# Where the low part of a weight chunk starts in its buffer: 128 bytes away, modulo 256, from where the high part starts

## The chip, the cores and the metric

The kernel runs on one core of a Trainium2 chip. The core has a matrix engine (TensorE; in the profile PE for the matmul's stream of columns and PEld for the load of its stationary operand), a vector engine (DVE), a scalar engine (ACT), GpSimd (POOL) and a queue engine that only issues transfers (SP). The metric is the time of one execution on the device, in microseconds; of several executions the median counts.

## The reference

A two-layer model over 512 tokens of width 1024, all in float32. Layer 0 mixes tokens by dilated attention in three groups, layer 1 by an mLSTM; after each comes a SwiGLU feed-forward of inner width 2816. Cut to what matters:

```python
def dilated_attention_mixer(xn, positions, w_in, w_out):
    proj = (xn @ w_in).reshape(B, S, N_GROUPS, 3, ATTN_HEADS, ATTN_HEAD_DIM)   # q, k, v
    ...                                     # rope, windowed softmax per group, groups mixed
    return o.reshape(B, S, ATTN_WIDTH) @ w_out

def mlstm_mixer(xn, w_in, ...):
    proj = xn @ w_in
    ...                                     # conv, gates, chunked recurrence
    return (h * jax.nn.sigmoid(o_pre)) @ w_out

def swiglu(xn, w_in, w_out):
    gu = xn @ w_in
    return (jax.nn.silu(gu[..., :D_FF]) * gu[..., D_FF:]) @ w_out

for i in range(2):
    h = h + (dilated_attention_mixer, mlstm_mixer)[i](rms_norm(h, ...), ...)
    h = h + swiglu(rms_norm(h, ffn_norm[i]), ffn_w_in[i], ffn_w_out[i])
return rms_norm(h, final_norm)
```

Nearly all of the work is the products with the weight matrices.

## The kernel before, in words

**Products in three matmuls.** TensorE takes its operands in a shortened float format (`F32R`). To keep float32 accuracy every operand is split into a high part (a rounded copy, made by ACT) and a low part (the difference, made by DVE), and a product is three matmuls: high by high, high by low, low by high (`SPLITS`, line 47). So each weight chunk of 128 x 1024 numbers has two buffers, tag `whi` for the high part and `wlo` for the low part, three of each in rotation (`W_BUFS`). `split_chunk` (line 227) allocates both and issues the two splitting instructions.

**Where a chunk starts.** The buffers are longer than the chunk by `PAD` = 64 elements (256 bytes per partition), and a chunk starts at an offset in them: `WIDE` = 0, `NARROW` = 16 elements (64 bytes) or `TOKENS` = 48 elements (192 bytes). A buffer is 1088 x 4 = 4352 bytes = 17 x 256 long, so all buffers of a tag start at the same place modulo 256, and the high and the low part of a chunk do too. In the memory plan of the built program that place is 32, and nearly all activation tiles that are streamed start at 32 as well. `WIDE` chunks thus start at 32, `NARROW` ones at 96 and `TOKENS` ones at 224. Every fourth chunk of the attention goes to a spare pair of buffers (`spare`), without padding or offset, whose place in the plan is 96.

**Which products are narrow.** Several large products are done by a seven-product (Strassen-like) scheme on blocks; their operands are half as long, so a matmul has 256 columns and not 512. These are the q and k projections of the attention (`qk_unit`, matmul at line 1055, tiles `a0g1c`, `a1g1u` and so on), the feed-forward's first product in both layers (`products` in `ffn_in`, line 1677, tiles `f0j_c`, `f0j_p`, `f0j_u` in layer 0 and `f1j_*` in layer 1) and its second product in layer 0 (`tile_mm`, line 1993, tile `fo`, weights `f0P`). In all of them the weights are the stationary operand, loaded before each matmul (128 columns of 4 bytes per partition), and the activations are streamed (256 columns of 4 bytes). They use `NARROW`. The mLSTM's v projection (`project_tokens`, line 326, tiles `mv`) streams 256 columns of weights over stationary activations, and uses `TOKENS`. Everything else has 512 columns and uses `WIDE`.

**The order of one triple.** The innermost loop issues, for each k, the matmuls high weights by high activations, high weights by low activations, low weights by high activations. The weights of a matmul are loaded while the matmul ahead of it streams. Beside the first matmul of a triple runs the second load of the high part, beside the second matmul the load of the low part, and beside the third the load of the next high part:

```python
for m in range(2):
    for k in range(4):
        for a, b in SPLITS:       # (0, 0), (0, 1), (1, 0): 0 high, 1 low
            nc.tensor.matmul(acc[name][:, m * HALF:(m + 1) * HALF], whl[a][:, k, m * P:(m + 1) * P],
                             ops[okey][b][:, k], ...)
```

The steps in k and m are multiples of 256 bytes, so modulo 256 each load and each stream starts where its buffer's chunk starts.

**What sets the order.** The program is written out in full: a list of products per stage, with the splits of the chunk that comes two products later issued between them (`AHEAD`). Each engine works its list in order and waits on semaphores. Loads of raw weights are issued by SP and wait for free buffers.

Of the kernel before, what the change touches and what calls it, by code (L numbers as in the profile page):

```python
# [12 lines left out]
F32R = mybir.dt.float32r  # L13
# [4 lines left out]
P = 128  # L18
# [24 lines left out]
           (19, 20, 21))  # L43
LAST_OUTPUTS = {6: 22, 7: 23}
W_BUFS = 3
PAD, WIDE, NARROW, TOKENS = 64, 0, 16, 48
SPLITS = [(0, 0), (0, 1), (1, 0)]


# [27 lines left out]
def tile_hybrid_dilated_attn_mlstm(  # L77
# [5 lines left out]
    x = x[0]  # L83
    out = out[0]

    def pool(stack, name, **kw):
        return stack.enter_context(tc.tile_pool(name=name, bufs=1, **kw))
# [3 lines left out]
    wp = pool(ctx, "w")  # L91
# [116 lines left out]
    spare = []  # L208
    ahead_of_splits = [None]

    def behind_scores():
        return tc.issue_after(ahead_of_splits[0]) if ahead_of_splits[0] is not None else nullcontext()
# [3 lines left out]
    def behind_factors():  # L216
        return tc.issue_after(ahead_of_casts[0]) if ahead_of_casts[0] is not None else nullcontext()
    splits = itertools.count()
# [3 lines left out]
    def run_late(_):  # L222
        while lows:
            with tc.issue_after(last_on(mybir.EngineType.DVE)):
                lows.pop(0)()

    def split_chunk(chunk, at=WIDE):

        raw, n, view, name = chunk
        p, more, bufs = (spare[0], "4", 1) if spare and next(splits) % (W_BUFS + 1) == W_BUFS else (wp, "", W_BUFS)  # L230
        at, pad = (0, 0) if more else (at, PAD)
        hi = p.tile([P, 1024 + pad], F32R, tag="whi" + more, name=name + "_h", bufs=bufs)[:, at:at + 1024]
        lo = p.tile([P, 1024 + pad], F32R, tag="wlo" + more, name=name + "_l", bufs=bufs)[:, at:at + 1024]
        with behind_factors():
            nc.scalar.activation(hi[:, :n], raw[:, :n], AF.Copy)  # L235
        def low():
            nc.vector.tensor_tensor(lo[:, :n], raw[:, :n], hi[:, :n].bitcast(F32), op=ALU.subtract)  # L237
        if late[0]:
            lows.append(low)
        else:  # L240
            with behind_scores():
                low()
        return view(hi), view(lo)

    def split_weights(src, shape, name):
        return split_chunk(load_chunk(src, shape, name))
# [30 lines left out]
    def project(pairs, w2d, c0, nk, evac, name, hook=None, ready=(), amid=False):  # L277

        acc = [acc_tile("%s_%d" % (name, m)) for m in range(2)]
        for ch in range((nk + 3) // 4):  # L280
            n = min(4, nk - 4 * ch)
            whl = ready.pop(0) if ready else split_chunk(weight_chunk(w2d, ch, c0, n, "%s_k%d" % (name, ch)))
            for m in range(2):
                with fenced():
                    multiply(acc[m], whl, pairs, ch, m, nk)
                if 4 * ch + n == nk and hook is None:
                    evac(m, acc[m])
                if amid and (ch, m) == (1, 0):
                    with tc.issue_after(last_on_pe()):
                        run_deferred(lambda t: t <= tick[0] + 1)  # L290
            if 4 * ch + n == nk and hook is not None:
                hook()
                for m in range(2):
                    evac(m, acc[m])
            advance()
# [20 lines left out]
    def project_tokens(pairs, w2d, c0, evac, name, tok=lambda t, tb: t[:, tb * P:(tb + 1) * P]):  # L316

        acc = [acc_tile("%s_%d" % (name, m)) for m in range(2)]
        for ch in range(KC // 4):
            whl = split_chunk(weight_chunk(w2d, ch, c0, 4, "%s_k%d" % (name, ch)), TOKENS)  # L320
            for m in range(2):
                with fenced():
                    for i, k in itertools.product(range(2), range(4)):
                        kk = ch * 4 + k
                        for a, b in SPLITS:
                            nc.tensor.matmul(
                                acc[m][:, i * 256:(i + 1) * 256],
                                tok(pairs[a][kk], 2 * m + i), whl[b][:, k, :],
                                start=(kk == 0 and i == 0 and (a, b) == SPLITS[0]),
                                stop=(kk == KC - 1 and (a, b) == SPLITS[-1]),  # L330
                                skip_group_check=True)
                ends[name] = last_on_pe()
                if ch == KC // 4 - 1:
                    evac(m, acc[m])
            advance()
# [85 lines left out]
    with ExitStack() as actx:  # L421
# [93 lines left out]
            else:  # L515
                nc.scalar.activation(h[k], xps[k], AF.Copy)

        his = [wp.tile([P, 1024 + PAD], F32R, tag="whi", name="first%d_h" % i, bufs=W_BUFS)[:, :1024] for i in range(2)]
        los = [wp.tile([P, 1024 + PAD], F32R, tag="wlo", name="first%d_l" % i, bufs=W_BUFS)[:, :1024] for i in range(2)]
        facc = [ps.tile([P, 512], F32, tag="o", name="a0g0q_%d" % m, bufs=2) for m in range(2)]  # L520

        def v12_parts(pr):
# [953 lines left out]
    def norm(key, k0, name, ssum=None, wait=1):  # L1476
        pair = x_tiles(name)
        add = None
        if ssum is None:
            ssum, add = squares_of(name)  # L1480
        for k in range(KC):
            split_act(pair[0][k], pair[1][k], h[k], col(key, k0 + k))
            if add is not None:
                add(k)
        v = npl.tile([P, TB], F32, tag="rs_v4", name=name + "v", bufs=2)
        box = {}

        def sums():
            sp = ps.tile([P, 512], F32, tag="t", name=name + "ss", bufs=1)
            for tb in range(TB):  # L1490
                nc.tensor.matmul(sp[:, tb:tb + 1], ssum[:, tb * P:(tb + 1) * P], ones[:, 0:1],
                                 start=True, stop=True)
            nc.vector.tensor_copy(v, sp[:, :TB])
            box["finish"]()
        rbc, r, hook = inverse_rms(v, name, box)
        defer(wait, sums)
        return pair, rbc, r, hook
# [253 lines left out]
    def output_products(layer, fp, wo, sums_of_rows):  # L1751
# [7 lines left out]
        narrow = NARROW if sums_of_rows else WIDE  # L1759
# [10 lines left out]
        def subtract(out, x, y):  # L1770
            nc.vector.tensor_tensor(out, x, y, op=ALU.subtract)

        def split_operand(name, u, src):

            i = UNITS * (PARTS.index(name) % 3) + u
            nm = "f%d%s_%d" % (layer, name, u)
            if i < 2 * len(PRODUCTS):
                t = fp.tile([P, 2, 2, HALF], F32R, tag="op%d" % i, name=nm)
                hi, lo = t[:, 0], t[:, 1]
            else:  # L1780
                hi, lo = [fp.tile([P, 2, HALF], F32R, tag="gu0", name=nm, bufs=3) for _ in range(2)]
            nc.scalar.activation(hi, src, AF.Copy)
            subtract(lo, src, hi.bitcast(F32))
            ops[name, u] = [[t[:, k] for k in range(2)] for t in (hi, lo)]
# [18 lines left out]
        def prepare_first_sum(u, own, nm):  # L1803

            view = lambda t: t.rearrange("p (k n) -> p k n", k=2)
            hi = wp.tile([P, 1024 + PAD], F32R, tag="whi", name=nm + "_h", bufs=W_BUFS)[:, narrow:narrow + 1024]
            lo = wp.tile([P, 1024 + PAD], F32R, tag="wlo", name=nm + "_l", bufs=W_BUFS)[:, narrow:narrow + 1024]
            for t, ks in first_sums[u]:
                nc.scalar.activation(view(hi)[:, ks], t, AF.Copy)
                subtract(view(lo)[:, ks], t, view(hi)[:, ks].bitcast(F32))  # L1810
            whl["P5", u] = view(hi), view(lo)
            for t, ks in first_sums[u]:
                subtract(view(own)[:, ks], t, view(own)[:, ks])
            split_operand("P5", u, sums[u])

        def prepare_product(name, u):
# [22 lines left out]
            if sums_of_rows and name == "P5":  # L1839
                prepare_first_sum(u, t, nm)  # L1840
                return
# [98 lines left out]
        first, second = (0, 1) if sums_of_rows else (1, 0)  # L1940
# [6 lines left out]
        for e in order:  # L1947
            name, i = e.split("_")
# [29 lines left out]
    pair, rbc, _, hook = norm("ffn", 0, "n1", ssum)  # L1978
# [62 lines left out]
    with ExitStack() as mctx:  # L2041
# [142 lines left out]
        i = 0  # L2184
# [165 lines left out]
    pair, rbc, _, hook = norm("ffn", KC, "n3", ssum)  # L2350
# [224 lines left out]
```

## Time and profile before

| | |
|---|---|
| time, median of 3 runs (lowest to highest) | 1358.64 us (1357.73 to 1359.58) |
| the profiled execution: its own time | 1359.36 us |
| its span, first to last instruction | 1357.6 us |
| TensorE clock granted, mean | 0.998 |
| matmuls recorded | 9100 |
| of these with 256 columns: line 1677 / 1055 / 1993 / 326 | 3024 / 1848 / 840 / 192 |

A stage's pace is read from the start of one matmul to the start of the next. The duration in a row is longer than that (281 ns where a matmul starts every 118), since matmuls are pipelined: a row's duration includes the way through the array, and the next one starts meanwhile. In a table of windows the count of a window takes in the instructions that hang over its edges, so the pace is (window + duration of one) / count. PEld rows are the loads of stationary operands.

### The profile page before, as it was taken

How to read it: one execution, taken by the hardware profiler on the slowest of the kernel's cores; microseconds unless marked ns; L12 is line 12 of the kernel's file. 1: busy time of each engine (PE TensorE's matmuls, PEld its weight loads, DVE VectorE, ACT ScalarE, POOL GpSimd, SP SyncE). 2: the span in 40 equal slices, each digit the busy share in tenths (PEclk: the TensorE clock that was granted, in tenths of full speed). 3: DMA queues.
4: the chain of work that ended last, by engine and by line, in shares of the span. 5: the costliest groups of instructions: out<-in, count | busy, mean ns of one | idle time of the engine just before them, and what ended most of it. 6: DMA issues, size and time to landing. Idle time of an engine off the chain costs nothing. (4 is left out here: it accounts for less than half of the span.)

```text
span 1357.6 us, 23346 instructions
## 1 busy us (share of the span) xinstructions
PE 1340.8 (99%) x9100; PEld 1232.5 (91%) x9100; DVE 1132.2 (83%) x1787; ACT 813.0 (60%) x1303; POOL 196.8 (14%) x272
## 2 busy tenths in 40 slices
PE   9999999999999999999999999999999999999997
PEld 7898899999998889999999998888888999999886
DVE  7988789798976499888878898898758988998887
ACT  6776576767664355544577464785534554558854
POOL 3000013141412001000010110123200112112113
PEclk9999999999999999999999999999999999999999
DMA  9354245455586357334351743324333545437863
GB/s 309 119 179 155 78 141 164 148 176 168 168 274 192 134 140 196 94 99 125 125 156 65 185 115 92 93 78 119 86 122 98 128 140 171 140 128 176 194 170 102
DMA packets 141271, 194.90 MB, mean 144 GB/s; under 512 B 9029, under 2 KB 106117, under 8 KB 141161
## 3 DMA queue, kind: packets, MB, share of 16 engines
q1 hardware_dynamic: 120128, 140.73, 32.9%
q0 software_dynamic: 19808, 52.48, 16.0%
q8 instruction: 71, 1.16, 0.4%
q10 hardware_dynamic: 1224, 0.21, 0.1%
q14 instruction: 40, 0.32, 0.1%
HBM read 167.30 MB, written 22.54 MB: 140 GB/s over the span
## 5 line engine op out<-in xcount | busy, mean ns | idle before, releaser
L1800 POOL DMA_DIRECT2D f0S<-in_ffn_w_out_dram x10 | 8.8, 891 | 251.5 <-DVE f0hid L1716 168.6
L2364 POOL DMA_DIRECT2D hD<-hB x32 | 20.7, 655 | 109.4 <-DVE hB L2361 109.2
L1825 POOL DMA_DIRECT2D f1T<-in_ffn_w_out_dram x15 | 17.8, 1186 | 86.1 <-ACT f1T L1828 41.0
L272 PE MATMUL mo<-n_h,mo_k_h 128*128 128x512 f32 x64 | 25.4, 397 | 0.0
L272 PE MATMUL mo<-n_h,mo_k_l 128*128 128x512 f32 x64 | 25.2, 394 | 0.0
L272 PE MATMUL awo<-ao_h,awo_k_h 128*128 128x512 f32 x64 | 25.2, 393 | 0.0
L272 PE MATMUL mqk<-n_h,mqk_k_h 128*128 128x512 f32 x64 | 25.1, 393 | 0.0
L272 PE MATMUL mo<-n_l,mo_k_h 128*128 128x512 f32 x64 | 25.1, 393 | 0.0
L272 PE MATMUL mwo<-yo_h,mwo_k_l 128*128 128x512 f32 x64 | 25.1, 392 | 0.0
L272 PE MATMUL mqk<-n_l,mqk_k_h 128*128 128x512 f32 x64 | 25.1, 392 | 0.0
L272 PE MATMUL mwo<-yo_l,mwo_k_h 128*128 128x512 f32 x64 | 25.1, 392 | 0.0
L272 PE MATMUL f0j<-n_h,f0j_h 128*128 128x512 f32 x64 | 25.0, 391 | 0.0
L272 PE MATMUL f1j<-n_h,f1j_h 128*128 128x512 f32 x64 | 25.0, 391 | 0.0
L272 PE MATMUL mwo<-yo_h,mwo_k_h 128*128 128x512 f32 x64 | 25.0, 391 | 0.0
L272 PE MATMUL mqk<-n_h,mqk_k_l 128*128 128x512 f32 x64 | 25.0, 390 | 0.0
L272 PE MATMUL awo<-ao_h,awo_k_l 128*128 128x512 f32 x64 | 25.0, 390 | 0.0
L272 PE MATMUL awo<-ao_l,awo_k_h 128*128 128x512 f32 x64 | 25.0, 390 | 0.0
L272 PE MATMUL f0j<-n_h,f0j_l 128*128 128x512 f32 x64 | 24.9, 390 | 0.0
L272 PE MATMUL f1j<-n_h,f1j_l 128*128 128x512 f32 x64 | 24.9, 390 | 0.0
L272 PE MATMUL f0j<-n_l,f0j_h 128*128 128x512 f32 x64 | 24.9, 389 | 0.0
L272 PE MATMUL f1j<-n_l,f1j_h 128*128 128x512 f32 x64 | 24.9, 389 | 0.0
L237 DVE TENSOR_TENSOR v1P_l<-v1W,v1P_h 128x1024 fp32r<-128x1024 f32 x14 | 17.1, 1224 | 9.2 <-ACT v1P_h L235 9.1
(2746 smaller groups left out, 6011.9 us busy)
## 6 DMA issues: line engine op xcount, KB each, us to landing
f0j_w<-in_ffn_w_in_dram SPq DMA_DIRECT2D x17, 512.0 KB, 5.9
f1j_w<-in_ffn_w_in_dram SPq DMA_DIRECT2D x17, 512.0 KB, 6.7
f1T<-in_ffn_w_out_dram POOLq DMA_DIRECT2D x15, 512.0 KB, 6.5
f0hid<-in_ffn_w_in_dram SPq DMA_DIRECT2D x9, 512.0 KB, 5.2
f1hid<-in_ffn_w_in_dram SPq DMA_DIRECT2D x9, 512.0 KB, 5.0
v0W<-in_attn_w_in_dram SPq DMA_DIRECT2D x8, 512.0 KB, 6.4
v1W<-in_attn_w_in_dram SPq DMA_DIRECT2D x8, 512.0 KB, 4.0
awo_k_w<-in_attn_w_out_dram SPq DMA_DIRECT2D x8, 512.0 KB, 3.9
```

The lines of the kernel that those rows point to most:

```text
L237: nc.vector.tensor_tensor(lo[:, :n], raw[:, :n], hi[:, :n].bitcast(F32), op=ALU.subtract)
L272: nc.tensor.matmul(acc, whl[a][:, k, m * P:(m + 1) * P], pairs[b][kk], start=(kk == 0 and (a, b) == SPLITS[0]), stop=(kk == nk - 1 and (a, ...
L1800: nc.gpsimd.dma_start(t, src[1][:, ks], accum_op=ALU.add)
L1825: nc.gpsimd.dma_start(view(to), weight_rows(hk * UNITS + u, n), accum_op=ALU.add)
L2364: nc.gpsimd.dma_start(hD[k // 4].rearrange("(b i) x -> i b x", i=R)[:, :, c0:c0 + R], t[R * a_:R * (a_ + 1)])
```

## The change

Each offset becomes a pair, one for the high and one for the low part. `WIDE` stays at 0 for both. `NARROW` becomes 16 elements for the high part and 48 for the low part: the low part starts at 224 modulo 256 and not at 96. `TOKENS` becomes 48 and 16: the low part starts at 96 and not at 224. The allocation of a pair moves into a helper, `weights_tiles`. The tags, their sizes and their numbers stay, and every buffer has its old address; the spare pair stays without offset.

```diff
-PAD, WIDE, NARROW, TOKENS = 64, 0, 16, 48
+PAD, WIDE, NARROW, TOKENS = 64, (0, 0), (16, 48), (48, 16)
...
+    def weights_tiles(name, at=WIDE):
+        return [wp.tile([P, 1024 + PAD], F32R, tag="w" + x, name=name + "_" + x[0], bufs=W_BUFS)[:, o:o + 1024]
+                for x, o in zip(("hi", "lo"), at)]
+
     def split_chunk(chunk, at=WIDE):
 
         raw, n, view, name = chunk
-        p, more, bufs = (spare[0], "4", 1) if spare and next(splits) % (W_BUFS + 1) == W_BUFS else (wp, "", W_BUFS)
-        at, pad = (0, 0) if more else (at, PAD)
-        hi = p.tile([P, 1024 + pad], F32R, tag="whi" + more, name=name + "_h", bufs=bufs)[:, at:at + 1024]
-        lo = p.tile([P, 1024 + pad], F32R, tag="wlo" + more, name=name + "_l", bufs=bufs)[:, at:at + 1024]
+        if spare and next(splits) % (W_BUFS + 1) == W_BUFS:
+            hi, lo = [spare[0].tile([P, 1024], F32R, tag="w%s4" % x, name=name + "_" + x[0]) for x in ("hi", "lo")]
+        else:
+            hi, lo = weights_tiles(name, at)
...
-            hi = wp.tile([P, 1024 + PAD], F32R, tag="whi", name=nm + "_h", bufs=W_BUFS)[:, narrow:narrow + 1024]
-            lo = wp.tile([P, 1024 + PAD], F32R, tag="wlo", name=nm + "_l", bufs=W_BUFS)[:, narrow:narrow + 1024]
+            hi, lo = weights_tiles(nm, narrow)
```

The first two chunks of the kernel, which were allocated by hand, go through the helper too, at offset 0 as before. The built program has the same instructions in the same order on every engine, with the same waits on them; only the start of the low part in `NARROW` and `TOKENS` chunks differs.

More of the change, by code (lines that the diff above doesn't have):

```diff
@@ L516, in x_keep @@
                 nc.scalar.activation(h[k], xps[k], AF.Copy)
-        his = [wp.tile([P, 1024 + PAD], F32R, tag="whi", name="first%d_h" % i, bufs=W_BUFS)[:, :1024] for i in range(2)]
-        los = [wp.tile([P, 1024 + PAD], F32R, tag="wlo", name="first%d_l" % i, bufs=W_BUFS)[:, :1024] for i in range(2)]
+        his, los = zip(*(weights_tiles("first%d" % i) for i in range(2)))
         facc = [ps.tile([P, 512], F32, tag="o", name="a0g0q_%d" % m, bufs=2) for m in range(2)]
```

## The prediction

> **What bounds the kernel now.** I read the page's totals first, then the windows of whole stages, then the rows of single tiles, then the timeline.
>
> ```profile
> span 1357.6 us, 23346 instructions
> PE 1340.8 (99%) x9100; PEld 1232.5 (91%) x9100; DVE 1132.2 (83%) x1787; ACT 813.0 (60%) x1303; POOL 196.8 (14%) x272
> PEclk9999999999999999999999999999999999999999
> ```
>
> TensorE streams for 1340.8 of 1357.6 us at full clock, so the kernel ends when its matmuls end, and only the pace of the matmuls, or a new wait, can move the time. Next the windows of the same stage in both layers (1512 matmuls of 256 columns each, line 1677): window, its length, busy time and count of each engine, clock.
>
> ```profile
> 521.70:700.00 178.30, 178.30 (x1514) 178.24 (x1513) 150.38 (x152) 97.16 (x122) 3.92 (x4) 1.00 0.41 125
> 1071.60:1243.50 171.90, 171.90 (x1515) 171.86 (x1514) 154.62 (x160) 96.87 (x123) 30.58 (x44) 1.00 0.46 143
> ```
>
> The same list of matmuls takes 178.3 us in layer 0 and 171.9 us in layer 1. TensorE never idles in either window and the clock is 1.00 in both, so the matmuls themselves have two paces. Inside the stages:
>
> ```profile
> 530.00:690.00 160.00, 160.00 (x1360) 160.00 (x1360) 1.00 0.39 116
> 1085.00:1240.00 155.00, 155.00 (x1370) 155.00 (x1369) 1.00 0.47 149
> L1677 PEld LDWEIGHTS f0j_u<-f0T2h,f0j4S_h x8: 187/188/188, 527.5 to 530.0; 128*128 128x128 f32 x8
> L1677 PE MATMUL f0j_u<-f0T2h,f0j4S_h x8: 281/281/281, 527.6 to 530.1; 128*128 128x256 f32 x8
> L1677 PEld LDWEIGHTS f0j_u<-f0T2l,f0j4S_h x8: 192/192/192, 527.6 to 530.1; 128*128 128x128 f32 x8
> L1677 PEld LDWEIGHTS f0j_u<-f0T2h,f0j4S_l x8: 187/188/188, 527.7 to 530.2; 128*128 128x128 f32 x8
> ...
> L1677 PE MATMUL f1j_u<-f1T3h,f1j4S_h x8: 276/276/276, 1083.0 to 1085.3; 128*128 128x256 f32 x8
> L1677 PEld LDWEIGHTS f1j_u<-f1T3l,f1j4S_h x8: 187/188/188, 1083.0 to 1085.3; 128*128 128x128 f32 x8
> ```
>
> With the durations of the tile rows, the pace is (160.00 + 0.281) / 1360 = 117.85 ns in layer 0 and (155.00 + 0.276) / 1370 = 113.34 ns in layer 1. I call them the long and the short pace; they differ by 4.5 ns a matmul, or 13.5 ns a triple. In the long pace one load of each triple is stretched from 188 to 192 ns; in the short pace none is. The shapes are the same, and so is the distance that the change alters (start of the weights loaded next, minus start of the stream, modulo 256): 96 - 32 = 64 for every load in both stages. So 64 allows both paces, and something else picks one:
>
> ```profile
> 1077.21 0.28 PE L1677 MATMUL f1j_p<-f1T1l,f1j4S_h 128*128 128x256 f32 x1
> 1077.33 0.28 PE L1677 MATMUL f1j_p<-f1T1h,f1j4S_l 128*128 128x256 f32 x1
> 1077.45 0.33 PE L1677 MATMUL f1j_u<-f1T2h,f1j4S_h 128*128 128x256 f32 x1
> 1077.62 0.28 PE L1677 MATMUL f1j_u<-f1T2l,f1j4S_h 128*128 128x256 f32 x1
> ...
> 1078.42 0.28 PE L1677 MATMUL f1j_u<-f1T2h,f1j4S_l 128*128 128x256 f32 x1
> 1078.54 0.28 PE L1677 MATMUL f1j_u<-f1T2h,f1j4S_h 128*128 128x256 f32 x1
> 1078.65 0.28 PE L1677 MATMUL f1j_u<-f1T2l,f1j4S_h 128*128 128x256 f32 x1
> ```
>
> Layer 1 also starts in the long pace (0.12 apart at 1077.2). One matmul then comes 0.17 us after the one before it, and within six matmuls the steps are 0.113. The short pace then holds for the remaining 1460 matmuls of the stage. Layer 0 has no such hiccup and stays long to its end. I read this as a cycle in time: in the long pace three matmuls in a row start at three offsets against some fixed beat, each of them a little late, and come back to the first; a start at the right offset repeats itself, and is the short pace.
>
> **What the distance does.** The trace has the same effect where the load cannot be the limit, under 512 columns, at three distances. The tail of a stage at distance 0, then the attention's output with a spare buffer (64), then the last v projection with a spare buffer (weights stream from 96, activations load at 32, so 192):
>
> ```profile
> 1250.00:1330.00 80.00, 80.00 (x354) 66.26 (x354) 1.00 0.77 173
> 437.30 0.40 PE L272 MATMUL awo<-ao_h,awo_k_h 128*128 128x512 f32 x1
> 440.80 0.39 PE L272 MATMUL awo<-ao_h,awo_k_h 128*128 128x512 f32 x1
> 412.10 0.39 PE L357 MATMUL a3g12v<-a3g12v_k_l,xa_h 128*128 128x512 f32 x1
> 416.90 0.39 PE L357 MATMUL a3g12v<-a3g12v_k_l,xa_h 128*128 128x512 f32 x1
> ```
>
> Distance 0: (80.00 + 0.39) / 354 = 227.1 ns. Distance 64, first and last row of 15 steps: 3.50 / 15 = 233.3 ns. Distance 192, 21 steps: 4.80 / 21 = 228.6 ns. So beside a 512-column stream a load at 64 costs some 6 ns and one at 192 some 1.5 ns. These are short stretches, and of 512 columns; no row has 256 columns with a load at 192.
>
> The Trainium skill speaks against any effect: TensorE: Matmul & The Clock Gate, section Step-by-step: what each phase is for, says that the stream and the stationary load have independent read ports and that loading the next weights takes no bandwidth from the running matmul. By it the distance is free and the time stays. The rows above, 233.3 against 227.1 ns with the same shapes, differ from it.
>
> **The change, part by part.** No instruction is added, removed or moved, and no wait. ACT and DVE write the same number of bytes to the same buffers, at another offset:
>
> ```profile
> L237 DVE TENSOR_TENSOR mwo_k_l<-mwo_k_w,mwo_k_h 128x1024 fp32r<-128x1024 f32 x8 | 9.8, 1223 | 8.3 <-ACT mwo_k_h L235 8.1
> L237 DVE TENSOR_TENSOR mv_k_l<-mv_k_w,mv_k_h 128x1024 fp32r<-128x1024 f32 x8 | 9.7, 1217 | 0.0
> L237 DVE TENSOR_TENSOR a0g2P_l<-a0g2W,a0g2P_h 128x1024 fp32r<-128x1024 f32 x7 | 8.6, 1222 | 2.3 <-ACT a0g2P_h L235 2.3
> ```
>
> A low part takes 1223 ns at 32, 1217 at 224 and 1222 at 96, so I take 0 for the writes. What changes is one load in three: in the built program 1784 of the 5695 loads that run beside a 256-column stream of lines 1677, 1993 and 1055 go from 64 to 192, always the load beside the second matmul of a triple (spare buffers leave out some of the attention). The other two stay at 64.
>
> I forecast that the long pace ends everywhere. It needs three late starts in a row that lead back to the first. One of the three loads now disturbs less (1.5 against 6 ns), so the cycle no longer closes; the starts wander until one hits the right offset, and there the short pace repeats itself, if a load at 192 lets it. Matmuls at the long pace, counted by starts 116 ns or more apart:
>
> ```profile
> 705.00:755.00 50.00, 50.00 (x427) 50.00 (x426) 1.00 0.38 91
> L1993 PE MATMUL fo<-f0P,f0P_0w_h x112: 281/281/281, 700.0 to 790.1; 128*128 128x256 f32 x112
> L1055 PE MATMUL a0g1c<-xa_h,a0g1P_h 128*128 128x256 f32 x16 | 4.5, 281 | 0.0
> L1055 PE MATMUL a0g2c<-xa_h,a0g2P_h 128*128 128x256 f32 x16 | 4.4, 276 | 0.0
> ```
>
> - Line 1677: all 1512 in layer 0 and the first 51 in layer 1: 1563 x 4.5 ns = 7.0 us.
> - Line 1993: all 840 (50.28 / 427 = 117.8 ns): 3.8 us.
> - Line 1055: 879 of 1848 (rows with 281 are long, with 276 short): 4.0 us.
> - Together 14.8 us.
>
> What of it is lost again: the cover is the work of DVE, which must keep up with a faster TensorE. For line 1677 it does, since layer 1 already runs the short pace with 154.62 us of DVE in 171.90. In two places it hardly does:
>
> ```profile
> 780.00:800.00 20.00, 20.00 (x172) 20.00 (x172) 19.59 (x26) 13.50 (x18) 0.00 (x0) 1.00 0.46 133
> 800.00:810.00 10.00, 10.00 (x64) 8.98 (x64) 10.00 (x14) 5.98 (x9) 0.96 (x1) 1.00 0.38 106
> 276.00:314.00 38.00, 37.31 (x317) 36.73 (x317) 35.52 (x51) 26.74 (x43) 13.09 (x20) 1.00 0.65 189
> ```
>
> From 780 to 810 DVE is busy 29.6 of 30 us, so I count nothing of the 0.9 us that some 200 long matmuls would give there. In the attention's long stretches DVE works 35.5 of 38 us and TensorE already has short waits (0.7 of 38 us idle); I take a third of the 4.0 us off, 1.3. For the starts that still wander after each wait I take 0.3.
>
> `TOKENS` (192 matmuls, now streamed from 224 and from 96 in turn):
>
> ```profile
> 866.00:870.70 4.70, 4.70 (x44) 4.70 (x43) 1.00 0.39 115
> ```
>
> They run at 4.976 / 44 = 113.1 ns, the short pace, and have nothing to win but their few long steps (29, 0.1 us). Bounds of the cost: 0, and 64 triples at 13.5 ns = 0.9 us; I take the middle, 0.4.
>
> Sum: 14.8 + 0.1 - 0.9 - 1.3 - 0.3 - 0.4 = 12.0 us. The profiled execution took 1359.36 us (span 1357.6), which gives 1347.4; against the median of 1358.64, which is 0.7 below it, **1346.6 us**. If nothing is lost it is 1343.7; if all of line 1993 and half of the attention are lost, 7 + 2 = 9 us remain, 1349.6.
>
> **The rivals.**
>
> *The short pace breaks (slower).* The place is the second matmul of each triple where the short pace rules now: 1461 in layer 1, 969 in the attention, 163 at line 326. What a load has to spare there is small, as rows of 128 columns show, where only the load limits:
>
> ```profile
> 188.21 1.95 PE L788 MATMUL a0s<-a0g_k,a0g_q 128*128 128x128 f32 x16
> ```
>
> With the last one's 275 ns off, 15 steps take 1.675 us: 111.7 ns. The short pace of 113.3 leaves 1.7 ns; from a delay of 1.7 ns at distance 192 on, the next matmul starts late and the offset is lost. The 512-column rows give 1.5 ns, hardly less, and theirs is a mean of steps that differ. The price is 13.5 ns a triple: 2593 x 4.5 = 11.7 us, so 1370.3 us if the long stretches stay long; if those gain half, 1363. For it speaks the thin margin; against it that the short pace held under distance 0 (512 columns) and 64 (256 columns) alike, so that the right offset seems not to depend on the distance.
>
> *Nothing changes.* The two loads that stay at 64 keep the cycle closed, and the short stretches stay: 1358.6. The stretched load, beside the first matmul in layer 0, keeps its 64, which speaks for it; in the attention it sits at other places of the triple. The skill's rule of independent ports would give this time too.
>
> *One middle pace everywhere.* Two of three loads late: two thirds of 4.5 ns on all 5,920 matmuls is 17.8 us where now 14.9 are paid; at half of 4.5, 13.3. So 1357 to 1361.6.
>
> **How the numbers follow.** All short: 0.60, around 1346.6, own range 1343.5 to 1350. Short pace broken: 0.20, 1362 to 1371. Nothing: 0.10. Middle pace or a mixture of stretches: 0.10, half of it 1350 to 1356. The range reaches from 1343 to 1366, which leaves out the upper half of the second case and a little below. A measurement tells 0.2%, 2.7 us, from no change. Faster by more: 0.60 + 0.05 = 0.65. Within: 0.10 + 0.04 = 0.14. Slower by more: 0.20 + 0.01 = 0.21.
>
> **What would show it.** Right: the MATMUL rows of lines 1677 and 1993 read 276 in layer 0 too, no stationary load reads 192 in these stages, the window of layer 0's stage falls from 178.3 to some 172 us, and the rows at 780 to 810 show first idle time of TensorE. Wrong: 281 in layer 1 (the short pace broke), or 281 still in layer 0 with 192 at the same loads (nothing changed). A time near 1347 with 281 in layer 0 would mean that the gain came from elsewhere.

## The result, and the profile after

The changed kernel takes 1349.96 us (median of 9 runs, 1348.85 to 1352.58), the kernel before 1358.93 us beside it (median of 9, 1350.94 to 1366.78). The ratio is 0.9932, 95% interval 0.9907 to 0.9956. The profiled execution of the changed kernel took 1350.34 us, span 1348.6. The forecast was 1346.6.

First the totals of the page of the changed kernel: same numbers of instructions, 11.7 us less of TensorE, the same clock.

```profile
span 1348.6 us, 23346 instructions
PE 1329.1 (99%) x9100; PEld 1219.9 (90%) x9100; DVE 1131.8 (84%) x1787; ACT 812.8 (60%) x1303; POOL 196.6 (15%) x272
PEclk9999999999999999999999999999999999999999
```

Then its windows over the feed-forward's seven-product stage in layer 0 and in layer 1 (window, its length, busy time and count of PE, PEld, DVE, ACT, POOL, clock, DMA share, GB/s):

```profile
521.70:693.40 171.70, 171.70 (x1513) 171.46 (x1512) 149.91 (x152) 97.13 (x122) 3.90 (x4) 1.00 0.43 129
1062.20:1233.90 171.70, 171.70 (x1514) 171.48 (x1513) 154.37 (x160) 96.59 (x122) 30.61 (x44) 1.00 0.47 143
```

Layer 0 now takes what layer 1 takes and took, some 172 us; from its first matmul to the first of the next stage it takes 171.8 us, and took 178.1. Below, rows of one tile of that stage, which read 281 for the matmuls and 192 for one load in three before:

```profile
L1680 PEld LDWEIGHTS f0j_u<-f0T2h,f0j4S_h x8: 187/188/188, 527.0 to 529.4; 128*128 128x128 f32 x8
L1680 PE MATMUL f0j_u<-f0T2h,f0j4S_h x8: 276/276/277, 527.1 to 529.5; 128*128 128x256 f32 x8
L1680 PEld LDWEIGHTS f0j_u<-f0T2l,f0j4S_h x8: 188/188/188, 527.1 to 529.5; 128*128 128x128 f32 x8
L1680 PEld LDWEIGHTS f0j_u<-f0T2h,f0j4S_l x8: 187/188/188, 527.2 to 529.6; 128*128 128x128 f32 x8
```

And the rows of the second product's line, also 281 before:

```profile
L1995 PE MATMUL fo<-f0P,f0P_0w_h x112: 275/276/277, 693.4 to 780.9; 128*128 128x256 f32 x112
```

The sum by stages, from the first matmul of each to the first of the next, in the two profiled executions:

| stage | before, us | after, us | gain | forecast |
|---|---|---|---|---|
| up to layer 0's seven-product stage (attention) | 521.95 | 521.66 | 0.3 | 2.7 |
| line 1677/1680, layer 0 | 178.1 | 171.8 | 6.3 | 6.8 |
| line 1993/1995 and the tail of its stage | 109.9 | 107.1 | 2.8 | 2.9 |
| mLSTM (with `TOKENS`) | 261.8 | 261.7 | 0.1 | -0.3 |
| line 1677/1680, layer 1 | 171.6 | 171.7 | -0.1 | 0.2 |
| the rest, to the end of the span | 114.1 | 114.6 | -0.4 | 0 |
| starts that wander, in all stages | | | (above) | -0.3 |
| sum | 1357.6 | 1348.6 | 9.0 | 12.0 |

The gain came where the forecast put it, but for the attention.

One thing the table cannot show: the executions of the kernel before fall into three groups. Of the 82 that ran beside the kernels of this study, 5 took 1350.9 to 1351.9 us, 58 took 1357.1 to 1361.1, and 19 took 1364.5 to 1367.8. The third group lies 6.4 us above the second (medians 1365.7 and 1359.3), which is what the long pace costs in one seven-product stage (178.1 against 171.6 us); the first lies 7.7 below it. The nine executions of the changed kernel form one group. The experiments below say why.

### The profile page after: what moved, and what is told of

The parts are those of the page before. It is cut to its first block, busy times and chain, and to the rows that moved or that the text cites. A ratio compares the mean times of both kernels' runs of the same rounds, so it can differ in the third digit from the quotient of the medians.

```text
span 1348.6 us, 23346 instructions
## 1 busy us (share of the span) xinstructions
PE 1329.1 (99%) x9100; PEld 1219.9 (90%) x9100; DVE 1131.8 (84%) x1787; ACT 812.8 (60%) x1303; POOL 196.6 (15%) x272
```

## The experiments

The theory after the result (called A in the expectations): a start at the right offset repeats itself and gives the short pace, at distance 64 as well; three late starts repeat each other and give the long pace; the offset (the moment of a start against some beat) after a wait decides which; and the change only makes the long pace unable to repeat. The rivals: the load at 192 is itself what makes a matmul quick, so each triple needs it; or a distance has a price of its own, whatever the others are.

### Only the moment of a start moves, no address

The kernel with all chunks at 64, and one more matmul at the head of each of the nine j of layer 0's stage (a j is 168 matmuls: seven products of 24):

```diff
-PAD, WIDE, NARROW, TOKENS = 64, (0, 0), (16, 48), (48, 16)
+PAD, WIDE, NARROW, TOKENS = 64, (0, 0), (16, 16), (48, 48)
+EXTRA = 128
...
+                if layer == 0 and key == "A11":
+                    nc.tensor.matmul(acc[name][:, :EXTRA], whl[0][:, 0, :P], ops[okey][0][:, 0, :EXTRA],
+                                     start=True, stop=False, skip_group_check=True)
```

> Every chunk at (16, 16) and TOKENS at (48, 48), as before the change, with one more matmul of 128 columns ahead of the first product of each of the nine j in layer 0's stage (its sum is overwritten by the next matmul): only the moment of the next start moves, no address. Theory A (the offset of a start picks the pace): at least one of the nine entries reaches the short pace, which holds at least to the next extra matmul; between 1350 and 1358, plus 9 x 0.112 = 1.0 us for the extra matmuls. Rival B (addresses alone set the pace): 117.85 ns throughout the stage, 1358.7 + 1.0 = 1359.7.

It took 1356.14 us (1354.67 to 1362.94, 10 runs). Windows of the second to the fifth j in its profile:

```profile
541.40:561.10 19.70, 19.70 (x170) 19.70 (x169) 16.31 (x17) 9.89 (x12) 0.00 (x0) 1.00 0.44 141
561.30:580.30 19.00, 19.00 (x170) 19.00 (x169) 16.11 (x17) 9.92 (x12) 0.00 (x0) 1.00 0.36 112
580.40:600.20 19.80, 19.80 (x171) 19.80 (x170) 16.32 (x17) 9.89 (x12) 0.00 (x0) 1.00 0.34 108
600.30:619.30 19.00, 19.00 (x170) 19.00 (x169) 16.10 (x17) 9.91 (x12) 0.00 (x0) 1.00 0.33 101
```

The same work with the same addresses takes 19.7, 19.0, 19.8, 19.0 us: short in the first j, then long and short in turn through the other eight, each pace holding for the 168 matmuls to the next extra one. The difference, 0.7 to 0.8 us, is 168 x 4.5 ns = 0.76. Rival B of this run (addresses alone set the pace) is out. The offset of a start picks the pace, and both repeat themselves at distance 64.

The same extra matmuls, with `NARROW` at (16, 48):

> The kernel with the extra matmul of 128 columns at the head of each of the nine j of layer 0's stage, now with NARROW at (16, 48) (TOKENS at (48, 48)). With all chunks at 64 the nine stretches between the extra matmuls came out long and short in turn (118.1 and 113.8 ns). Theory A (with the pair the long pace is no closed cycle, so each disturbance is followed by the short pace within a few triples): all nine at 113.4 to 114, time 1350.2 + 1.0 = 1351.2. Rival C (the pair only moved the offset at the stage's entry): long and short in turn again, about 1355.5.

It took 1351.62 us (1350.70 to 1352.23, 4 runs). Windows of the third to the fifth j:

```profile
559.40:578.40 19.00, 19.00 (x170) 19.00 (x170) 16.23 (x17) 9.91 (x12) 0.00 (x0) 1.00 0.38 118
578.60:597.60 19.00, 19.00 (x170) 19.00 (x169) 16.14 (x17) 9.91 (x12) 0.00 (x0) 1.00 0.35 112
597.70:616.70 19.00, 19.00 (x170) 19.00 (x169) 16.23 (x17) 9.90 (x12) 0.00 (x0) 1.00 0.33 104
```

Every j is short. The same nine disturbances no longer lead into the long pace: with the pair it does not repeat itself.

### One chunk with the pair

All chunks at (16, 16) and `TOKENS` at (48, 48), but for the first chunk of layer 0's seven-product stage:

```diff
-PAD, WIDE, NARROW, TOKENS = 64, (0, 0), (16, 48), (48, 16)
+PAD, WIDE, NARROW, TOKENS = 64, (0, 0), (16, 16), (48, 48)
+ENTRY = (16, 48)
...
-                return split_chunk((w[key], 1024, ..., nm + key), NARROW)
+                return split_chunk((w[key], 1024, ..., nm + key),
+                                   ENTRY if (layer, s, key) == (0, 0, "A11") else NARROW)
```

> Every chunk at (16, 16) and TOKENS at (48, 48), as before the change, but for one: the first chunk of the feed-forward's seven-product stage of layer 0 has (16, 48), so 8 of 9100 loads lie at distance 192. Theory A (a start at the right offset repeats itself; the pair only breaks the cycle of the long pace): line 1680 in layer 0 and line 1995 run at 113.3 ns to the end, the time is 1349 to 1351. Rival B (each triple needs its load at 192 to keep the short pace): the long pace comes back after the first product, 1358.5.

Ten runs: six at 1350.9 to 1354.7, three at 1358.0 to 1360.1, one at 1366.5 (median 1353.49). So in most executions eight loads of 9100 are worth nearly as much as 1784: rival B is out. But the short pace did not always hold to the end. The profile was taken of the slowest execution; its timeline shows where it was lost:

```profile
533.25 0.28 PE L1682 MATMUL f0j_c<-f0B21l,f0j4A_h 128*128 128x256 f32 x1
533.36 0.28 PE L1682 MATMUL f0j_c<-f0B21h,f0j4A_l 128*128 128x256 f32 x1
533.67 0.39 PE L1682 MATMUL f0j_u<-f0T3h,f0j4S_h 128*128 128x256 f32 x1
533.89 0.28 PE L1682 MATMUL f0j_u<-f0T3l,f0j4S_h 128*128 128x256 f32 x1
...
534.58 0.28 PE L1682 MATMUL f0j_u<-f0T3h,f0j4S_h 128*128 128x256 f32 x1
534.69 0.28 PE L1682 MATMUL f0j_u<-f0T3l,f0j4S_h 128*128 128x256 f32 x1
534.81 0.28 PE L1682 MATMUL f0j_u<-f0T3h,f0j4S_l 128*128 128x256 f32 x1
534.93 0.28 PE L1682 MATMUL f0j_u<-f0T3h,f0j4S_h 128*128 128x256 f32 x1
```

Short (0.11) to 533.36; then come three waits, with steps of 0.31, 0.22 and 0.21 us, and from there the steps are 0.12. They stay so to the end of the stage. The changed kernel has the same wait at the same place:

```profile
532.45 0.28 PE L1680 MATMUL f0j_c<-f0B21h,f0j4A_l 128*128 128x256 f32 x1
532.73 0.38 PE L1680 MATMUL f0j_u<-f0T3h,f0j4S_h 128*128 128x256 f32 x1
532.95 0.28 PE L1680 MATMUL f0j_u<-f0T3l,f0j4S_h 128*128 128x256 f32 x1
533.07 0.39 PE L1680 MATMUL f0j_u<-f0T3h,f0j4S_l 128*128 128x256 f32 x1
533.29 0.28 PE L1680 MATMUL f0j_u<-f0T3h,f0j4S_h 128*128 128x256 f32 x1
533.41 0.28 PE L1680 MATMUL f0j_u<-f0T3l,f0j4S_h 128*128 128x256 f32 x1
533.53 0.28 PE L1680 MATMUL f0j_u<-f0T3h,f0j4S_l 128*128 128x256 f32 x1
533.64 0.28 PE L1680 MATMUL f0j_u<-f0T3h,f0j4S_h 128*128 128x256 f32 x1
533.76 0.28 PE L1680 MATMUL f0j_u<-f0T3l,f0j4S_h 128*128 128x256 f32 x1
533.87 0.28 PE L1680 MATMUL f0j_u<-f0T3h,f0j4S_l 128*128 128x256 f32 x1
```

Here two steps after the wait are 0.12, and from 533.53 on they are 0.113 (0.34 for three). In that slowest execution of the one-chunk kernel, layer 1's stage was long too, with the same code as before the change (178.0 us from its first start to its last). That is the third group of the kernel before, as far as one profile can say; no profile was taken of the kernel before itself in its first or third group.

### The pair in one product of seven

```diff
-PAD, WIDE, NARROW, TOKENS = 64, (0, 0), (16, 48), (48, 16)
+PAD, WIDE, NARROW, TOKENS = 64, (0, 0), (16, 48), (48, 48)
...
-                return split_chunk((w[key], 1024, ..., nm + key), NARROW)
+                return split_chunk((w[key], 1024, ..., nm + key),
+                                   NARROW if key == "A11" else (16, 16))
```

> The pair (16, 48) stays in the attention and in line 1995, but in the feed-forward's first product it holds for one chunk in seven, that of the first product of each j; the other six have (16, 16). TOKENS at (48, 48). Theory A (the short pace repeats itself at distance 64 as well, and the pair is needed only to come back to it after a wait): short pace in both layers but for the rest of a j in which TensorE had to wait, some 70 matmuls at 4.5 ns or 0.3 us a layer; 1350.5 to 1351, narrow spread. Rival B (the short pace needs the pair in each product): long in six of seven products, 0.86 x 13.6 = 11.7 us more, 1362.

It took 1350.52 us (1348.93 to 1351.21, 6 runs), and in its profile both seven-product stages are short throughout (171.7 and 171.5 us), with six of seven products at 64. The pair is a way back after a wait, and is not needed in between. Together with the three runs above it shows that the moment of a start picks the pace, and that the pair is what leads back after a wait. Against what beat the moment counts, no run here shows.

### Other distances

`NARROW` alone is altered, `TOKENS` stays at (48, 16); the kernel before, in the third row, has (48, 48) there. The paces are the mean steps over the seven-product stages of layers 0 and 1 in the profile, from the first start to the last, short waits included:

| `NARROW` | distances in a triple | time, us | mean steps, ns |
|---|---|---|---|
| (16, 48), the change | 64, 192, 64 | 1349.96 (1348.85 to 1352.58) | 113.6 and 113.5 |
| (48, 16) | 192, 64, 192 | 1352.46 (1349.96 to 1369.19) | 113.7 and 113.5 |
| (16, 16), before | 64, 64, 64 | 1358.93 (1350.94 to 1366.78) | 117.8 and 113.5 |
| (48, 48) | 192, 192, 192 | 1366.90 (1359.68 to 1368.85) | 117.8 and 117.8 |
| (16, 0) | 64, 0, 64 | 1367.67 (1366.80 to 1384.29) | 117.8 and 117.8 |
| (32, 32) | 128, 128, 128 | 1376.21 (1375.53 to 1376.57) | 120.0 and 120.0 |
| (0, 0) | 0, 0, 0 | 1376.58 (1375.61 to 1376.69) | 120.0 and 120.0 |

> NARROW at (48, 48), TOKENS at (48, 16): all three loads of a triple at distance 192. Theory A1 (what closes the cycle of the long pace is that three loads disturb alike; the mixture opens it): two paces remain, the stage of layer 0 at 117 to 118 ns in some executions, times spread between 1350 and 1366. Theory A2 (a load at 192 disturbs less than one at 64, as the 512-column rows say; the more of them the better): short pace everywhere, 1350.0. Rival D (192 itself breaks the short pace): slower than 1366.

> NARROW at (48, 16): the two loads of the high part of a triple at distance 192, the one of the low part at 64. Theory A1 (any mixture opens the cycle): 1350.0, as narrow a spread as the changed kernel. Theory A2 (fewer loads at 64 is what counts): 1350.0 too. Rival E (it must be the load beside the second matmul that leaves 64): long pace in layer 0 again, 1358.

> NARROW at (0, 0): all loads of a triple at distance 0, as in the 512-column stages, where 227.1 ns was the lowest of the three distances. Theory A1 (equal distances keep the cycle closed): two paces remain, spread between 1350 and 1366. Theory A2 (the disturbance by a load depends on the distance, and 0 is the mildest): short pace everywhere, 1350.0.

> NARROW at (32, 32): all three loads of a triple at distance 128. Equal distances have given two paces, 113.3 and 117.85 ns, at 64 and at 192, and one, 120.0 ns, at 0. Theory F (what counts is whether the load starts at another half of 256 bytes than the stream at 32: 128 then behaves like 64 or 192, with two paces): spread between 1350 and 1368. Theory G (128 behaves like 0, modulo 128): 120.0 ns everywhere, 1376. Theory H (128 is the distance without any disturbance): 113.3 ns everywhere, 1350.

> NARROW at (16, 0): the loads of the high part at 64, that of the low part at distance 0. Theory A (any mixture in the three loads opens the cycle, the short pace remains): 1350 to 1351, narrow spread, 113.3 ns in both layers. Rival I (a load at 0 is late at whatever offset, as under equal distances of 0, where all loads read 192 ns and the pace was 120.0): the short pace is lost, the triple takes at least one grid step of 6.67 ns more, 5920 / 3 x 6.67 = 13.2 us above the changed kernel's 1350, so 1363.

Equal distances of 0, in the window of layer 0's stage and in the rows of a tile:

```profile
530.00:690.00 160.00, 160.00 (x1336) 160.00 (x1335) 131.71 (x130) 81.08 (x99) 3.34 (x4) 1.00 0.39 115
```

```profile
L1680 PEld LDWEIGHTS f0j_u<-f0T2h,f0j4S_h x8: 192/192/192, 529.4 to 531.9; 128*128 128x128 f32 x8
L1680 PE MATMUL f0j_u<-f0T2h,f0j4S_h x8: 283/283/283, 529.5 to 532.0; 128*128 128x256 f32 x8
L1680 PEld LDWEIGHTS f0j_u<-f0T2l,f0j4S_h x8: 192/192/192, 529.5 to 532.0; 128*128 128x128 f32 x8
```

Now every load reads 192 and every matmul starts (160.00 + 0.283) / 1336 = 120.0 ns after the last, in both layers and in each of four runs within 1.1 us. At 128 the window has the same 1336 matmuls: theory G of that run, modulo 128. So there is a third pace; of the equal distances tried it belongs to 0 and 128. A stretched load is not what makes it: at 128, at the same 120.0 ns, nearly all loads of the stage read 188 to 190. Nor is it the start of a load by itself: in the v projection with `TOKENS` at (48, 48) the activations are loaded from 32, as the weights are here, beneath streams from 224, and the steps are 113 or 114 ns for the most part.

Equal distances of 192, layer 0 and layer 1:

```profile
530.00:690.00 160.00, 160.00 (x1360) 160.00 (x1360) 134.68 (x134) 83.65 (x104) 2.46 (x3) 1.00 0.39 115
1085.00:1240.00 155.00, 155.00 (x1318) 155.00 (x1317) 134.82 (x139) 79.17 (x98) 25.09 (x40) 1.00 0.44 137
```

The load beside the first matmul, which read 192 before the change:

```profile
L1680 PEld LDWEIGHTS f0j_u<-f0T2l,f0j4S_h x8: 188/188/188, 528.4 to 530.9; 128*128 128x128 f32 x8
```

Layer 0 is as before the change, with the same 1360 matmuls in 160 us, and yet its loads read 187 or 188 and none 192; layer 1, which was short before, is long: 1318 matmuls where the kernel before had 1370. Some stretches of the attention ran short in this kernel (in its last unit but three, 160 of 168 steps are under 116 ns, and only the chunks of the spare pair are at 64 there), so 192 allows both paces, as 64 does. A load at 192 is not milder than one at 64, and theory A2 of that run falls.

The mixture of 64 and 0 falls as well (theory A of that run): 117.8 ns in both layers, with 1360 matmuls in 160 us. And of the two mixtures of 64 and 192, only (16, 48) has a narrow spread. With (48, 16) the profiled execution has both stages short, but 1021 of the 1848 steps of the attention at 116 to 130 ns, against 175 in the changed kernel and 879 before; and its ten runs go from 1349.96 to 1369.19. So it is not any mixture that opens the cycle. Of those tried, only two loads at 64 and the one beside the second matmul at 192 did. Why this one and not its mirror, no run here shows.

### TOKENS

The changed kernel with `TOKENS` at (48, 48):

> The changed kernel with TOKENS back at (48, 48); NARROW stays (16, 48). Theory A (the pair slows the 192 matmuls of the mLSTM's v projection, which now run at 118 to 120 ns, by some 0.7 us): about 1349.3, and the rows of line 330 at 113 to 116 ns again. Rival (that stretch waits for other work anyway): 1350.0, with longer waits there.

It took 1350.23 us (1349.42 to 1351.71, 10 runs; ratio to before 0.9917, 0.9893 to 0.9940, which overlaps that of the changed kernel). One chunk-row of the v projection in the changed kernel:

```profile
856.20:861.70 5.50, 5.50 (x48) 5.48 (x47) 5.33 (x8) 4.58 (x8) 1.13 (x1) 1.00 0.35 98
```

and with `TOKENS` undone:

```profile
856.30:861.60 5.30, 5.30 (x48) 5.30 (x47) 5.13 (x8) 4.38 (x7) 1.13 (x1) 1.00 0.36 102
```

0.2 us lost per 48 matmuls: the pair does break the short pace here (a mean step of 117.9 ns and not 113.8). But the mLSTM as a whole, from its first v matmul to layer 1's stage, takes 212.1 us in the one and 212.2 in the other; without the pair the recurrence that follows waits that much longer (its `m1nb` 0.9 us for ScalarE and not 0.5, its `m2num` 0.4 for VectorE, a wait that the changed kernel does not list). The rival holds: the part of the change in `TOKENS` costs a pace and no time. A triple has the same distances here as in `NARROW`, twice 64 and once 192, and the pace goes the other way. What differs is that the streams' start alternates and the loads' does not, so the distance alone does not tell a pace.

### Where the attention's gain went

The attention back at (16, 16), all else as changed:

```diff
+ATT = (16, 16)
...
-            whl = split_chunk((b[src], 1024, four_k, "a%dg%d%s" % (pr, g, name)), NARROW)
+            whl = split_chunk((b[src], 1024, four_k, "a%dg%d%s" % (pr, g, name)), ATT)
```

> The changed kernel with the attention's chunks back at (16, 16), so that the pair holds in the feed-forward and in TOKENS alone. Theory A (the attention's gain of pace turned into waits for VectorE and gave nothing): 1350.0 within 0.5, the feed-forward's stage of layer 0 begins at 521.7 as in both kernels. Rival (it gave what the prediction counted, 2.7 us, and something else took it back): 1352.7, the stage begins some 2.7 us later.

It took 1350.66 us (1349.63 to 1351.26, 10 runs), 0.7 above the changed kernel and 0.4 above the kernel without `TOKENS` (1350.23), which ran beside it; the intervals of their ratios to the kernel before overlap. Layer 0's stage begins at 522.7 us, and in those two at 521.7 and 521.6. Even at (16, 16) the attention's pace is not fixed: 1083 of its steps lie at 116 to 130 ns here, and 879 in the profile before. So the pair in the attention gives 0.3 to 1 us, if anything, and not 2.7. Where the rest goes is seen in the four long stretches of q and k products (57 to 97, 200 to 239, 276 to 314 and 349 to 387 us; 155 us in all), as the sum over the windows. Before:

```profile
sum 155.00, PE 151.56 PEld 149.14 DVE 142.63 ACT 108.10 POOL 41.49; mean PE 37.89 PEld 37.28 DVE 35.66 ACT 27.03 POOL 10.37
```

After:

```profile
sum 155.00, PE 149.15 PEld 146.58 DVE 142.63 ACT 108.14 POOL 41.35; mean PE 37.29 PEld 36.65 DVE 35.66 ACT 27.03 POOL 10.34
```

All distances 0 (the fourth window from 351 to 389):

```profile
sum 155.00, PE 153.40 PEld 152.11 DVE 142.49 ACT 107.28 POOL 42.22; mean PE 38.35 PEld 38.03 DVE 35.62 ACT 26.82 POOL 10.56
```

TensorE's busy time in the same 155 us goes from 153.4 over 151.6 to 149.2, and VectorE's stays at 142.5 to 142.6: the same work of VectorE passes in the same time, whatever TensorE's pace. Over all 1848 matmuls, the time above 113.3 ns a step in steps under 130 ns (the pace) and in longer ones (the waits) is 10.9 + 5.3 us at distance 0, 4.0 + 9.0 before and 1.0 + 11.5 after. From before to after the pace gave 3.0 us, and the waits took 2.5 of them. Two of these waits, before:

```profile
PE a3g1u L1055 <- DVE a3g_k L1025: 0.9, 1, 0.9
PE a2g1u L1055 <- DVE a2g_k L1025: 0.6, 1, 0.6
```

and after:

```profile
PE a3g1u L1058 <- DVE a3g_k L1028: 1.4, 1, 1.4
PE a2g1u L1058 <- DVE a2g_k L1028: 0.8, 1, 0.8
```

To test it, VectorE's work in the attention was made less; the differences of weight blocks for the q and k products are left out:

```diff
             def less(out, x, y):
-                with behind_scores():
-                    nc.vector.tensor_tensor(b[out], b[x], b[y], op=ALU.subtract)
+                return
```

> The changed kernel (TOKENS at (48, 48)) with the 44 differences of weight blocks left out that VectorE makes for the attention's q and k products (4 per unit of 11, 128 x 1024 at some 1.22 us each, 54 us of VectorE in all); the products then use the plain blocks, so that part of the computation is not done. The matmuls, their addresses and their pace stay. From the first q and k matmul to the first matmul of the feed-forward's stage the changed kernel takes 464.2 us, of which 11.5 us are steps of 130 ns or more among the q and k matmuls. Theory A (VectorE's work sets the attention's length, which is why a faster pace gave nothing there): the waits go to a few us and the stage begins 5 to 9 us sooner, 1341 to 1345 us. Rival (another chain, ScalarE's or GpSimd's, sets it): the stage begins within 1 us of where it did, 1349 to 1350.

It took 1339.10 us (1338.93 to 1339.52, 4 runs), and the stage begins at 510.96: 10.6 us sooner than without the edit (521.6), more than expected. The windows of four stretches of the attention (from 57, 200, 260 and 330 us, as long as those above):

```profile
sum 155.00, PE 154.34 PEld 153.28 DVE 118.55 ACT 110.43 POOL 37.67; mean PE 38.58 PEld 38.32 DVE 29.64 ACT 27.61 POOL 9.42
```

TensorE now hardly waits, and the waits over all 1848 steps fall from 11.4 to 3.1 us. So in the attention the work of VectorE, with what waits for it, set the end. The run cannot separate VectorE's own time (1131.7 us busy before this edit, 1082.2 after it) from what hangs on a difference, since all of it went: ScalarE's wait for a finished one, and the order that holds it behind the scores. GpSimd's busy time fell too, from 196.7 to 187.2 us, with the same 272 instructions.

Of the kernels that leave nothing out, none is shown to be faster than the changed one: the best two, (48, 48) for `TOKENS` and the pair in one product of seven, lie within its interval.

## Why the prediction was right, and where it was not

**What bounds the kernel, and the two paces:** right. The two paces are two ways in which starts repeat, and the same addresses gave both in turn.

**That the long pace ends everywhere, and that the short pace holds with a load at 192:** right, but for the 175 long steps that are left in the attention. The stages of layer 0 and line 1995 came out within 0.5 and 0.1 us of their terms; 0.4 of the 0.5 are three waits at 532 to 533 us. All three rivals fell: the short pace did not break in layer 1 (171.7 us), no middle pace showed in these stages, and something did change. One of its signs says less than the prediction took it to say: no load reads 192 in the long stages of the kernel at (48, 48), so a load of 188 is no proof of the short pace.

**The reason for it was wrong in one step:** "One of the three loads now disturbs less (1.5 against 6 ns), so the cycle no longer closes". The prices were carried over from 512-column streams. With 256 columns, distance 0, the mildest there (227.1 ns), is the worst (120.0), and three loads at 192 have the same two paces as three at 64. What leaves the long pace without a return is this one combination; by the reading of the prediction, (48, 48) should have been at least as good as (16, 48), and it is 17 us slower. The forecast of the sign was right, on a premise that did not hold.

**The attention was mis-sized:** "I take a third of the 4.0 us off". Nine tenths were lost in the profiled executions, 0.3 us was left. The row for it stood in the prediction: VectorE busy 35.52 of 38.00 us, and TensorE idle for 0.7. In that window 0.6 us of the idle time is the wait for VectorE's `a2g_k`, shown above. So VectorE was not merely close to being the limit there: TensorE already waited for it, and a faster TensorE only waits longer. This one term is 2.4 of the 3.0 us by which the profiled sum of 12.0 missed 9.0.

**`TOKENS`:** the pace was lost as the upper bound had it (118 ns, some 0.2 us per 48 matmuls), and its 0.4 us did not reach the end. The prediction asked for the cover of every gain, and not for the cover of this loss.

**Line 1993:** 2.8 against 2.9 us, and in part by luck. The loss was sized right, 0.8 us against 0.9, but not its place. The prediction put all of it at 780 to 810, where VectorE was busy 29.6 of 30 us. In the changed kernel that stretch holds 0.3 us of it, in two waits at 790 us; the other 0.5 come at 741.6, where TensorE waits for ScalarE:

```profile
741.61 0.28 PE L1995 MATMUL fo<-f0P,f0P_4w_l 128*128 128x256 f32 x1
742.13 0.50 PE L1995 MATMUL fo<-f0P,f0P_4w_h 128*128 128x256 f32 x2 [0.24 <-ACT fo L2018]
```

The sign that was named for this place, first idle time of TensorE, did not show: in the windows of 780 to 790 and 790 to 800 us PE is busy for 10.00 of 10.00. A row lasts 276 ns where a matmul starts every 113, so a wait shorter than the difference shows in the steps and not as idle time.

**The rule of independent ports** (the Trainium skill, TensorE: Matmul & The Clock Gate, section Step-by-step: what each phase is for), by which loading the next weights takes no read bandwidth from the running matmul: the prediction drew from it that the distance is free, and the traces disagree with that. With the instruction list unchanged, the start of the loaded weights alone moved the mean step from 113.6 to 120.0 ns.

## What to carry to other kernels

When the same list of matmuls takes two times in two stages of one trace, or the executions fall into groups, look at single steps for a pace that repeats itself, and at the waits that let it change; judge a remedy by its spread as much as by its median. A gain of pace counts only in a stage where no other engine ends last: here an engine that was busy 93% beside a TensorE that already waited took nine tenths of it. And a price measured at one shape need not hold at another, as the 512-column prices did not here: test the distances on the shape itself.

## What was not expected of the hardware

- The three paces of a triple are 3 x 113.34 = 340.0, 3 x 117.85 = 353.6 and 3 x 120.0 = 360.0 ns: 13.6 and 20.0 above the first, close to two and three times 6.7 ns. Starts held to steps of about 6.7 ns would give such sums, but the single steps do not show it: in the long pace each is 117 to 119 ns, and at distance 128 they are 117, 120 and 123 ns in turn. What the beat is, these runs don't say.
- For 256 columns the four equal distances tried fit a period of 128 bytes: 0 and 128 give 120.0 ns, 64 and 192 both of the other paces. A mixture of 64 and 192 differs from either of them, so for mixtures 64 and 192 are not the same.
- One extra matmul of 128 columns flipped the pace of the 168 that follow, eight times in a row.
